# Holding the sums of squares behind the turned tokens in a two-layer decoder trunk

## The chip, the core and the metric

The kernel runs on one core of a Trainium2 chip. The metric is device time in microseconds (us) of one execution. Engines go by the profile's names: PE is TensorE (PEld its weight loads), DVE is VectorE, ACT is ScalarE, POOL is GpSimd, SP is the engine that issues most DMAs.

## The reference

Sixteen learned meta tokens are put ahead of 512 real ones, which gives 528 tokens of 2048 features in float32. Two layers follow. The first normalizes by the root mean square, projects, and runs multi-scale retention beside a complex diagonal state space (S5); the second does the same with gated linear attention. Each ends in an output projection and a residual sum, and a last normalization closes the trunk. The change concerns the first normalization alone:

```
def _rmsnorm(x, w):
    xf = x.astype(jnp.float32)
    y = xf * lax.rsqrt(jnp.mean(xf * xf, axis=-1, keepdims=True) + EPS)
    return (y * w.astype(jnp.float32)).astype(x.dtype)

h = concat(meta, x)                                   # (1, 528, 2048)
q, k, v, z_a, u, z_b = split(_rmsnorm(h, norm_ab_w) @ w_in_ab)
```

## The kernel before

The language used here takes a program written in plain order and lets a planner order the instructions of each engine: ready work first, earlier lines of the program first among the ready, and blocks marked with a high priority ahead of the rest. Each engine then runs its list in order. The planner also sets the waits.

The opening is this. Six tiles `xt` of 88 tokens x 2048 features are loaded in two halves of the features (L228 to L232), first the left halves of all six, then the right ones. For each of 16 blocks of 128 features (k) and each half of the tokens (hf), TensorE turns three tiles of 88 x 128 into one PSUM tile `pt` of 128 x 264 (L242; 96 transposes, 32 turned tiles). Four PSUM tiles rotate. ScalarE writes the high part `xh`, scaled by the norm's weight and rounded to the format of the fast passes (L245). VectorE writes the rest, `xl` (L246). A raw copy, by ScalarE for the first token half and VectorE for the second (L250, L252), goes to DRAM through POOL's queue (L253) for the residual sum later on.

The square root's part is kept out of the products: a projection is computed on unnormalized tokens, and its result is multiplied by `rb`, 1/rms of each token on all partitions. For `rb` the squares of each token are summed over whole rows of `xt`, three tiles on ScalarE (L262), three on VectorE (L260), written at the place in the program that follows the turning of the tokens and the copy of some weight vectors, `wv` (L256). Then come the mean (L263), the reciprocal root (`rsqrt`, L121 to L129), six small matmuls `pr` that spread it (L269) and two copies into `rb` (L271). The pool `p0` with the tokens is released behind them.

Products go by panels (`panel_steps`, L136): 128 columns of weights against all tokens, in four steps of four blocks. A step loads a weight tile `wr` (256 KB, L153, SP's queue), casts its high part on ScalarE (`wh`, L156), subtracts on VectorE (`wl`, L157), both with high priority, and issues 24 matmuls of 128 x 264 (L167). Three weight buffers and two accumulators rotate. The first panels are those of the S5 input; `u_out` multiplies an accumulator by `rb` (L298) and sets it free. Beside them VectorE computes the S5 parameters (L340 to L346 are helpers through which most of its work goes), which TensorE transposes (`pa`, L414; `pc`, L459; `pp`, L485) and later uses for small kernels (`pk`, L528). Their loads (L332 to L334, L443) use room that `p0` has left.

Of the kernel before, what the change touches and what calls it, by code (L numbers as in the profile page):

```python
# [13 lines left out]
AF = mybir.ActivationFunctionType  # L14
ALU = mybir.AluOpType
# [16 lines left out]
T = 8  # L32
# [9 lines left out]

# [1 line left out]
def host_tables():  # L44
# [33 lines left out]
def tile_hybrid(ctx: ExitStack, tc: tile.TileContext, d: dict, out: bass.AP, dbg=None):  # L78
# [20 lines left out]

# [1 line left out]
    cst = cpool.tile([P, P + GC], F32, name="cst")  # L101
# [16 lines left out]
    def rsqrt(pool, ms, shape, np_, tag):  # L118
        """(ms + eps) ** -0.5 for a small tile of mean squares"""
        v = pool.tile(shape, F32, name="rs_v", tag=tag + "v")  # L120
        V.tensor_scalar(v[:np_], ms, EPS, None, op0=ALU.add)  # L121
        y = pool.tile(shape, F32, name="rs_y", tag=tag + "y", bufs=2)
        V.tensor_scalar(y.bitcast(I32)[:np_], v.bitcast(I32)[:np_], -0.5, 1597463007.0, op0=ALU.mult, op1=ALU.add)
        for _ in range(3):
            t = pool.tile(shape, F32, name="rs_t", tag=tag + "t")
            V.scalar_tensor_tensor(t[:np_], y[:np_], -0.5, y[:np_], op0=ALU.mult, op1=ALU.mult)
            V.tensor_tensor(t[:np_], t[:np_], v[:np_], op=ALU.mult)
            y2 = pool.tile(shape, F32, name="rs_y", tag=tag + "y", bufs=2)
            V.scalar_tensor_tensor(y2[:np_], t[:np_], 1.5, y[:np_], op0=ALU.add, op1=ALU.mult)  # L129
            y = y2  # L130
        return y

# [1 line left out]
    WPRI = 3000  # L134

    def panel_steps(res, wsrc, row0, col, xs, tok0=0, x0=None):  # L136
        """psum [128, 2, 512] = W[row0:, col:col+128]^T @ xs, float32 through three exact passes"""
        nk = len(xs)
# [53 lines left out]

    # ================= tokens in, transposed, split =================
    NB = 6
# [62 lines left out]
    for t in range(NB):  # L257
        junk = p0.tile([TB, D], F32, name="junk", tag="junk", bufs=2)
        if t % 2:
            V.scalar_tensor_tensor(junk, xt[t], 1.0, xt[t], op0=ALU.mult, op1=ALU.mult, accum_out=ssq[:, t:t + 1])  # L260
        else:
            A.activation(junk, xt[t], AF.Square, accum_out=ssq[:, t:t + 1])  # L262
    V.tensor_scalar(ssq, ssq, 1.0 / D, None, op0=ALU.mult)  # L263
# [19 lines left out]

    # ================= S5 =================
    u_d = dpool.tile([NG * GC, T, NC8], F32, name="u_d")
# [32 lines left out]

    # -- discretization, on [32 pairs, (group parity, state)] --
    NQ = 32  # L320
# [58 lines left out]
    n = sm()  # L379
# [36 lines left out]

    # -- powers of a: pw[:, n, re/im, pair] --
    V.memset(pw[:, 0, 0, :], 1.0)
# [3 lines left out]
    def cmul(dst, a, b, n):  # L422
        """dst[n] = a[n] * b, complex on axis 2"""
        bb = [b[:, j:j + 1, :].to_broadcast([P, n, NPAIR]) if n > 1 else b[:, j:j + 1, :] for j in range(2)]
        for j in range(2):
            q = sd.tile([P, 4, NPAIR], F32, name="cm", tag="cm", bufs=2)[:, :n]
            tt(q, a[:, :, 1, :], bb[1 - j], ALU.mult)
            tt(dst[:, :, j, :], a[:, :, 0, :], bb[j], ALU.mult)
            tt(dst[:, :, j, :], dst[:, :, j, :], q, ALU.add if j else ALU.subtract)
# [8 lines left out]

    # -- discretized input matrix, output matrix transposed --
    bt = [sd.tile([P, NPAIR, GC], F32, name="bt", tag="tmp", bufs=3) for j in range(2)]  # L440
# [26 lines left out]

    # -- chunk-end states from within the chunk --
    def pwv(j, ps_):
# [22 lines left out]
    sk = sk_cm.__enter__()  # L492
    # -- kernel of the lags within a chunk, output matrices times powers --
    zero = sk.tile([P, T * GC], F32, name="zero")
# [56 lines left out]
    r0b = r0b_cm.__enter__()  # L551
    # -- states across chunks: slot c becomes the state after chunk c --
    for c in range(1, NC8 - 1):
# [52 lines left out]

    # ================= residual stream, output projection =================
    def out_proj_panel(wsrc, row0, os, m, tok0=0):
# [11 lines left out]
    def split(pool, src, n, tag, bufs, scale=None):  # L620
        """an operand as the exact sum of two parts that the fast passes carry"""
        oh = pool.tile([P, n], F32R, name="oh", tag=tag + "h", bufs=bufs)
        ol = pool.tile([P, n], F32R, name="ol", tag=tag + "l", bufs=bufs)
        A.copy(oh, src)
        tt(ol, src, oh.bitcast(F32), ALU.subtract)
        return oh, ol
# [4 lines left out]
    def stacked(pool, name, n):  # L631
        """a 16-row operand's parts on three row groups, zeros between: one fast pass makes the three products"""
        t = pool.tile([SK, n], F32R, name=name)
        V.tensor_copy(t, zcol[:SK].to_broadcast([SK, n]))
        return t

    def stack_a(t, src, scale=None):
        """rows (high, high, low)"""
        for rows in (S0, S1):
            if scale is None:  # L640
                A.copy(t[rows], src)
            else:
                A.activation(t[rows], src, AF.Copy, scale=scale)
        if scale is None:
            tt(t[S2], src, t.bitcast(F32)[S0], ALU.subtract)
        else:
            stt(t[S2], src, scale, t.bitcast(F32)[S0], ALU.mult, ALU.subtract)

    def stack_b(t, src):
        """rows (high, low, high)"""  # L650
        for rows in (S0, S2):
# [13 lines left out]

    # ================= retention =================
    def rope(col, decay=None):
# [20 lines left out]
    def ret_panels(hd, order="kqvvzz", after=lambda n: None):  # L688
        """a head's projections, one panel for each letter"""
        vtm = vtm3  # L690
# [32 lines left out]
    def ret_mix(hd, k_, q_, vt, vtm, sz):  # L723
        # keys, token-major, decayed to the end of their chunk
        kw = r0b.tile([P, NCH - 1, P], F32, name="kw", tag="kw", bufs=1)
# [5 lines left out]
        stack_a(kwm3, pt[:META, 3 * P:], kdecm[:META, hd:hd + 1])  # L731
        # scores, transposed: [key, query]
        st = r0b.tile([P, NCH, P], F32, name="st", tag="st", bufs=2)
# [9 lines left out]
        stack_a(stm3, stm)  # L743
        # states and outputs, token-major
        on = r0b.tile([P, NCH, RDV], F32, name="on", tag="on", bufs=1)
# [100 lines left out]

    # ================= S5: gelu, gated linear unit =================
    r1p_cm = tc.tile_pool(name="r1p", bufs=1, side="right", reuse_waits="tile")
# [70 lines left out]

    # ================= layer 1: gated linear attention =================  # L920
    w_in = d["w_in_c"][0]
# [4 lines left out]

    # -- the low-rank gate code: the weights' high parts, then their low parts, in two passes --
    accg = psm.tile([P, 2, 512], F32, name="accg", tag="mm")
# [7 lines left out]
    opool_cm.__exit__(None, None, None)  # L936
    # -- 1 / rms of every token, along the free axis on all partitions --
    pq = mx("pq")
# [40 lines left out]
    def last_weights(f4):  # L979
        """the last projection's weights, split, where the tokens were"""  # L980
        for k in range(4):
# [9 lines left out]
    def last_norm():  # L991
        """the final norm's weight on all partitions"""
        for f4, (tag, bufs) in enumerate((("k", 2), ("k", 2), ("b", 2), ("b", 2))):
# [3 lines left out]
    def turn_group(f4):  # L997
        """the residual of 512 features, token-major, in place: chunk c in tile 4 f4 + c"""
        pts = []
# [11 lines left out]
    def evac(parts, src):  # L1011
        """a value, or its high and its low part"""
        if len(parts) == 1:
# [5 lines left out]
    def products(o, pairs):  # L1019
        """the sum of a^T b, of values in float32 or through the parts that the fast passes carry"""  # L1020
        todo = []
# [39 lines left out]
    for hd in range(GH):  # L1061
        # gates: cumulative log decay (times 16) within every chunk
        bs = []
# [34 lines left out]
        if done is not None:  # L1098
            O = gate(*done)
        # scores [key, query]: every pair of positions in the level where they part  # L1100
        st = gt("st", "st", 1, [P, SEQ])
# [29 lines left out]
        for lv, sz in enumerate((64, 32, 16, 8, 4, 2)):  # L1131
# [22 lines left out]
            place(sz, lv, pl)  # L1154
        # decays to the chunk's end for keys, from its start for queries
        parts = 2 if hd < GH - 1 else 1
# [45 lines left out]
        for z in zs:  # L1202
            A.activation(z, z, AF.Silu)
        # states and outputs, token-major
        if parts == 2:
# [53 lines left out]

    # ================= last projection, token-major; final norm =================  # L1260
    ssq = gt("ssq", "ssq", 1, [P, NCH, 4])
# [51 lines left out]
```

## Time and profile before

| what | value |
|---|---|
| time, median of 3 runs | 2174.68 us (2173.01 to 2177.08) |
| span of the profiled execution | 2173.9 us |
| PE busy | 2106.5 us, 97% |
| DVE busy | 1160.2 us, 53% |
| ACT busy | 803.2 us, 37% |
| moved by DMA | 223.72 MB, mean 103 GB/s |

The profiled execution lies inside the three runs: no other time of it is told than its span, which is 0.8 us below the median. The busy share of PE is an average over the whole run; its first slices are thinner than the rest, and those are the ones to look into.

### The profile page before, as it was taken

What the parts mean: (1) busy time and instruction counts of PE and PEld (TensorE: products, weight loads), DVE (VectorE), ACT (ScalarE), POOL (GpSimd) and SP (SyncE); (2) the same over time, 40 slices, a digit from 0 to 9 for tenths busy, and PEclk for the clock granted to TensorE, in tenths of its full rate; (3) what the DMA queues carried; (4) which work ended last, traced back from release to release, by engine and by line L of the source; (5) the groups of instructions that cost most, each with busy time, mean ns of one, the idle gap of its engine ahead of it and who ended that gap; (6) DMA issues with size and microseconds to landing.
All of it is one profiled execution on the core that took longest, in us unless ns stands there. A gap on an engine that the chain in (4) does not pass through costs nothing.

```text
span 2173.9 us, 39751 instructions
## 1 busy us (share of the span) xinstructions
PE 2106.5 (97%) x16052; PEld 1947.0 (90%) x16052; DVE 1160.2 (53%) x2452; ACT 803.2 (37%) x1536; POOL 71.7 (3%) x110
## 2 busy tenths in 40 slices
PE   6998988999999999999999999999999999999998
PEld 5997887999999999999999998988798889889776
DVE  5886871534344433445444566545834573555376
ACT  5333422543332333234323354344325333533343
POOL 3100012000000000000000020000000000000000
PEclk9999998999999999999999999999999999999999
DMA  7855437652323222322333322223232223233232
GB/s 232 216 119 146 135 96 238 194 164 78 89 74 92 78 79 86 90 77 80 93 92 92 93 80 73 79 68 83 78 88 68 83 79 88 68 83 89 82 117 78
DMA packets 391374, 223.72 MB, mean 103 GB/s; under 512 B 45990, under 2 KB 375030, under 8 KB 391062
## 3 DMA queue, kind: packets, MB, share of 16 engines
q1 hardware_dynamic: 383062, 208.10, 34.0%
q0 software_dynamic: 8096, 13.07, 2.2%
q8 instruction: 126, 2.06, 0.4%
q14 instruction: 58, 0.48, 0.1%
q10 hardware_dynamic: 32, 0.01, 0.0%
HBM read 193.15 MB, written 27.92 MB: 102 GB/s over the span
## 4 chain that ended last, share of the span: by engine, by line
PE 81%; issue 8%; DMA 4%; DVE 3%; ACT 2%; SPq 1%; POOL 0%; ACTq 0%; DVEq 0%; POOLq 0%
PE acc L167 69%; PE last L1271 2%; PE po L1029 2%; PE pl L1152 1%; DMA x_d<-St 1%; DMA xt<-in_x_dram 1%; DVE wl L157 1%; PE pkv L1029 1%; DMA y_d<-Y 1%; PE po L767 1%; DMA wr<-in_w_out_c_dram 1%; PE po L766 1%; ACT wh L156 1%; PE pkv L758 0%; DMA wr<-in_w_in_ab_dram 0%
## 5 line engine op out<-in xcount | busy, mean ns | idle before, releaser
L156 ACT CAST wh<-wr 128x512 fp32r<-128x512 f32 x608 | 375.7, 620 | 1011.0 <-PE acc L167 872.5
L167 PE MATMUL acc<-xh,wh 128*128 128x264 f32 (+1 forms) x3200 | 734.6, 300 | 3.6 <-ACT wh L156 3.6
L167 PE MATMUL acc<-xh,wl 128*128 128x264 f32 (+1 forms) x3200 | 730.7, 299 | 7.5 <-DVE wl L157 7.5
L167 PE MATMUL acc<-xl,wh 128*128 128x264 f32 (+1 forms) x3200 | 729.3, 299 | 0.0
L157 DVE TENSOR_TENSOR wl<-wr,wh 128x512 fp32r<-128x512 f32 x608 | 417.1, 687 | 543.4 <-ACT wh L156 522.5
L167 PEld LDWEIGHTS acc<-xh,wl 128*128 128x128 f32 x3200 | 509.4, 189 | 29.4 <-DVE wl L157 12.1
L167 PEld LDWEIGHTS acc<-xh,wh 128*128 128x128 f32 x3200 | 510.9, 189 | 23.6 <-ACT wh L156 4.8
L167 PEld LDWEIGHTS acc<-xl,wh 128*128 128x128 f32 x3200 | 513.1, 189 | 19.4 <-issue 0.4
L167 PE MATMUL acc<-oh,wh 128*128 128x264 f32 x896 | 181.9, 284 | 0.5 <-DVE sz L343 0.5
L167 PE MATMUL acc<-oh,wl 128*128 128x264 f32 x896 | 181.8, 284 | 0.0
L167 PE MATMUL acc<-ol,wh 128*128 128x264 f32 x896 | 181.8, 285 | 0.0
L343 DVE TENSOR_TENSOR h<-acc,h 128x528 f32<-128x528 f32 (+1 forms) x144 | 100.9, 700 | 143.8 <-PE acc L167 143.3
L167 PEld LDWEIGHTS acc<-oh,wh 128*128 128x128 f32 x896 | 139.0, 189 | 0.7 <-issue 0.7
L167 PEld LDWEIGHTS acc<-ol,wh 128*128 128x128 f32 x896 | 138.7, 188 | 0.0
L167 PEld LDWEIGHTS acc<-oh,wl 128*128 128x128 f32 x896 | 138.7, 188 | 0.0
L343 DVE TENSOR_TENSOR vf<-acc,rb 128x528 f32<-128x528 f32 x32 | 22.6, 707 | 44.8 <-PE acc L167 44.7
L912 POOL TENSOR_TENSOR sqa<-sqa,s 128x528 f32<-128x528 f32 x13 | 17.3, 1329 | 883.8 <-ACT s L911 883.8
L1141 ACT ACTIVATE E<-E 128x512 f32<-128x512 f32 x48 | 29.7, 629 | 32.8 <-DVE E L343 32.6
L343 DVE TENSOR_TENSOR E<-b 128x256 f32<-128x256 f32 (+1 forms) x112 | 41.0, 409 | 0.0
L1152 PEld LDWEIGHTS pl<-qh,E 128*64 128x64 f32 x704 | 26.3, 137 | 12.2 <-issue 4.3
L343 DVE TENSOR_TENSOR E<-E,k 128x512 f32<-128x512 f32 (+1 forms) x56 | 36.3, 668 | 0.0
L242 PE MATMUL pt<-cst,xt 88*128 88x88 f32 x96 | 17.0, 315 | 16.8 <-DMA xt<-in_x_dram 8.9
(430 smaller groups left out, 2147.3 us busy)
## 6 DMA issues: line engine op xcount, KB each, us to landing
wr<-in_w_in_ab_dram SPq DMA_DIRECT2D x256, 256.0 KB
wr<-in_w_in_c_dram SPq DMA_DIRECT2D x192, 256.0 KB
wr<-in_w_out_ab_dram SPq DMA_DIRECT2D x96, 256.0 KB
wr<-in_w_out_c_dram SPq DMA_DIRECT2D x64, 256.0 KB
xT_d<-raw POOLq DMA_DIRECT2D x32, 132.0 KB, 3.7
h<-xT_d SPq DMA_DIRECT2D x16, 264.0 KB
k_d<-zero SPq DMA_DIRECT2D x8, 512.0 KB
ca_d<-CA SPq DMA_DIRECT2D x32, 128.0 KB
```

Of the source, the lines that this page charges most:

```text
L156: A.copy(wh, wr)
L157: V.tensor_tensor(wl, wr, wh.bitcast(F32), op=ALU.subtract)
L167: PE.matmul(o, a[:, k, :], b[:, cols], start=(kk == 0 and pi == 0), stop=(kk == nk - 1 and pi == 2))
L242: PE.transpose(pt[:, j * TB:(j + 1) * TB], xt[hf * 3 + j][:, k * P:(k + 1) * P], ident[:TB, :TB])
L343: V.tensor_tensor(o, a, b, op=op)
L766: PE.matmul(po[:, :RDV], st[:, c, :], vt[:, c, :], start=True, stop=False)
L767: PE.matmul(po[:, :RDV], q_[:, toks(c)], S, start=False, stop=True)
L912: (G if m < KT - 2 else V).tensor_tensor(sqa, sqa, s, op=ALU.add)
L1029: PE.matmul(o, a, b, start=(n == 0), stop=(n == len(todo) - 1))
L1141: A.activation(e, e, AF.Exp, scale=1.0 / 16)
L1152: PE.matmul(pl[r:r + 64, c * 64:(c + 1) * 64], kh[j][:, c * P + r:c * P + r + 64], qh[j][:, c * 64:(c + 1) * 64], start=(j == 0), stop=(j ...
L1271: PE.matmul(acc, a[:, cs_], b, start=(k == 0 and pi == 0), stop=(k == 3 and pi == 2))
```

## The change

Each of the six instructions that square a token tile is handed to `keep_in_program_order`. The call adds an edge of order, without a wait, from the instruction to the one that the program traced just before it on the same engine. For the first square on ScalarE that is the last `xh` (L245, block 15, second half), for the first on VectorE the copy of `wv` (L256), and for the others the square before them on their engine. The planner may no longer put a square earlier in an engine's list. Before, it was free to do so once the token tile was loaded.

```
@@ -257,9 +257,10 @@
     for t in range(NB):
         junk = p0.tile([TB, D], F32, name="junk", tag="junk", bufs=2)
         if t % 2:
-            V.scalar_tensor_tensor(junk, xt[t], 1.0, xt[t], op0=ALU.mult, op1=ALU.mult, accum_out=ssq[:, t:t + 1])
+            i = V.scalar_tensor_tensor(junk, xt[t], 1.0, xt[t], op0=ALU.mult, op1=ALU.mult, accum_out=ssq[:, t:t + 1])
         else:
-            A.activation(junk, xt[t], AF.Square, accum_out=ssq[:, t:t + 1])
+            i = A.activation(junk, xt[t], AF.Square, accum_out=ssq[:, t:t + 1])
+        tc.keep_in_program_order(i)
     V.tensor_scalar(ssq, ssq, 1.0 / D, None, op0=ALU.mult)
     rs = rsqrt(cpool, ssq, [TB, NB], TB, "rs0")
```

The other hunks of the diff only take comments out. Line numbers behind L262 grow by one.

## Rows read from the trace of the kernel before

**Rows 1.** The page, part 1: busy us, share of the span, instructions.
```profile
PE 2106.5 (97%) x16052; PEld 1947.0 (90%) x16052; DVE 1160.2 (53%) x2452; ACT 803.2 (37%) x1536; POOL 71.7 (3%) x110
```
**Rows 2.** The chain that ended last, first 100 us: start us, us, what.
```profile
13.56 13.50 DMA xt<-in_x_dram
27.05 1.74 ACT junk L262
...
32.15 3.37 PE acc L167 x15
...
47.47 4.91 PE acc L167 x39
```
**Rows 3.** Busy us (instructions) by stretch: PE, PEld, DVE, ACT, POOL; clock, DMA share, GB/s.
```profile
20.45:30.24 9.79, 3.64 (x19) 2.62 (x19) 8.09 (x14) 8.96 (x16) 2.81 (x7) 1.00 0.94 324
30.24:36.00 5.76, 5.76 (x31) 5.76 (x30) 4.38 (x10) 3.09 (x9) 2.57 (x5) 1.00 0.96 341
...
47.00:60.00 13.00, 12.59 (x103) 12.17 (x102) 11.06 (x35) 2.68 (x6) 2.91 (x9) 1.00 0.47 147
60.00:72.40 12.40, 12.40 (x106) 12.40 (x104) 11.60 (x56) 4.66 (x8) 0.00 (x0) 1.00 0.81 156
```
**Rows 4.** The same for instructions on the turned tiles pt alone: PE, PEld, DVE, ACT.
```profile
0.00:17.50 17.50, 3.73 (x15) 2.29 (x15) 2.10 (x5) 2.83 (x7) 1.00 0.66 170
17.50:20.45 2.95, 2.90 (x15) 2.18 (x15) 2.61 (x8) 1.99 (x5) 1.00 1.01 301
20.45:30.24 9.79, 3.64 (x18) 2.61 (x18) 3.84 (x10) 3.34 (x9) 1.00 0.94 324
...
0.00:60.00 60.00, 17.01 (x96) 12.36 (x96) 19.71 (x48) 19.18 (x48) 1.00 0.70 219
```
**Rows 5.** The instructions that square the tokens: duration ns min/median/max, first and last start.
```profile
L262 ACT ACTIVATE junk<-xt x3: 1896/1897/1898, 20.2 to 27.0; 88x2048 f32<-88x2048 f32 x3
L260 DVE SCALAR_TENSOR_TENSOR junk<-xt x3: 2276/2277/2280, 20.7 to 48.9; 88x2048 f32<-88x2048 f32 x3
L262 ACT ACTIVATION_READ_ACCUMULATOR junk<-xt x3: 188/190/190, 22.0 to 28.8; 88x1 f32 x3
L260 DVE DVE_READ_ACCUMULATOR junk<-xt x3: 78/78/80, 22.9 to 51.2; 88x1 f32 x3
```
**Rows 6.** The timeline of SP's queue: start us, us, what it issued.
```profile
15.89 6.89 SPq L153 DMA_DIRECT2D wr<-in_w_in_ab_dram  x3
22.83 0.59 SPq L233 DMA_DIRECT2D cst<-in_cst_dram  x1
...
58.31 0.33 SPq L332 DMA_DIRECT2D lr<-in_s_lam_re_dram  x1
```
**Rows 7.** SP's waits from 15 to 31 us: total us, times, longest us.
```profile
SPq L153 <- DMA wr<-in_w_in_ab_dram: 5.3, 1, 5.3
```
**Rows 8.** The timeline of all engines where the products begin.
```profile
29.57 0.61 ACT L156 CAST wh<-wr 128x512 fp32r<-128x512 f32 x1
...
30.24 0.81 PE L167 MATMUL acc<-xh,wh 128*128 128x264 f32 x2
```
**Rows 9.** The timeline of DVE around rb; in brackets idle time before and its releaser.
```profile
48.81 0.21 DVE L256 COPY wv<-pv 128x64 f32<-128x64 f32 x1
48.94 2.28 DVE L260 SCALAR_TENSOR_TENSOR junk<-xt 88x2048 f32<-88x2048 f32 x1
...
58.32 0.43 DVE L271 COPY rb<-pr 128x264 f32<-128x264 f32 x1 [0.32 <-PE pr L269]
...
60.53 1.16 DVE L298 TENSOR_TENSOR ut<-acc,rb 128x264 f32<-128x264 f32 x2 [0.38 <-PE acc L167]
```
**Rows 10.** The timeline of PE at two later stops.
```profile
73.78 0.24 PE L414 MATMUL pa<-cst,abf 32*128 32x32 f32 x1 [1.11 <-DVE abf L343]
...
170.48 0.60 PE L528 MATMUL pk<-CA,bbD 128*32 128x128 f32 x2 [7.34 <-DVE CA L343]
```
**Rows 11.** Busy us by stretch around the second stop, columns as in rows 3.
```profile
165.00:170.00 5.00, 0.00 (x0) 0.00 (x0) 1.83 (x4) 0.88 (x2) 0.00 (x0) 0.54 0.60 111
170.00:175.00 5.00, 4.52 (x20) 4.16 (x21) 2.83 (x5) 1.81 (x3) 0.00 (x0) 0.50 0.42 104
```

More of the change, by code (lines that the diff above doesn't have):

```diff
@@ L259, in tile_hybrid @@
         if t % 2:
-            V.scalar_tensor_tensor(junk, xt[t], 1.0, xt[t], op0=ALU.mult, op1=ALU.mult, accum_out=ssq[:, t:t + 1])
+            i = V.scalar_tensor_tensor(junk, xt[t], 1.0, xt[t], op0=ALU.mult, op1=ALU.mult, accum_out=ssq[:, t:t + 1])
         else:
-            A.activation(junk, xt[t], AF.Square, accum_out=ssq[:, t:t + 1])
+            i = A.activation(junk, xt[t], AF.Square, accum_out=ssq[:, t:t + 1])
+        tc.keep_in_program_order(i)
     V.tensor_scalar(ssq, ssq, 1.0 / D, None, op0=ALU.mult)
```

## The prediction

> **What bounds the kernel now.** I read the page first, then the chain of waits over the first 100 us, then busy times by stretch, then the instructions one by one. The page says that TensorE is busy 97% of the span [rows 1], so as a whole the kernel is bound by products, and only a stage in which TensorE stands still can give much. The change touches such a stage. From 20.45 to 30.24 us TensorE works 3.64 of 9.79 us, while ScalarE works 8.96 and VectorE 8.09; from 30.24 to 36 and from 60 to 72.4 it has no gap at all, and from 47 to 60 only 0.41 us [rows 3]. So whatever is won or lost before 30 us is carried by TensorE up to 72 us.
>
> What fills ScalarE in the thin stretch? The three squares there cost 1.90 + 0.19 us each, the two on VectorE (L260, the third stands at 48.94) 2.28 + 0.08 us each [rows 5, 9]: 6.27 us of ScalarE's 8.96 and 4.72 us of VectorE's 8.09. TensorE's transposes need the PSUM tiles that these two engines empty, so each square holds the transposes up.
>
> But the squares are not the only thing that is late there. The chain shows the tokens' DMA still landing until 27.06 us (13.56 + 13.50) and a square right behind it [rows 2]. And the weights are late too: SP issues the first three weight tiles from 15.89 on and the tables at 22.83, is free at 23.42, and its next weight load then waits 5.3 us for a weight tile to land [rows 6, 7], so the first weights are in SBUF at about 28.8 us. ScalarE casts them at 29.57 and the first product can follow at 30.24 [rows 3, 8]. The squares delay this cast by 0.8 us at most.
>
> **The change, part by part.** Nothing is added or removed: the same six squares, the same DMAs. The mark ties each square to the instruction traced just before it on its engine, by order alone: ScalarE's first to the last scaled copy of a turned tile, VectorE's first to the copy of the weight vectors (L256), the others each to the last one before. Three things follow.
>
> *1. The thin stretch.* 6.27 us of ScalarE and 4.72 us of VectorE come free between 20 and 29 us. A turned tile (three transposes) costs ScalarE 19.18/32 = 0.60 us, VectorE 19.71/32 = 0.62 us and TensorE 3 x 17.01/96 = 0.53 us [rows 4]. In the run before, 15 + 15 + 18 = 48 transposes, 16 of 32 tiles, are through by 30.24 us [rows 4]. Free of squares the three could take 17 tiles (eight feature blocks, both halves, and one half of the ninth) before the last token block lands at 27.06; the 18th needs that block. From then on at 0.62 us a tile there is room for four more by 29.57. So at the first product the lead is between 1 tile (the planner puts the casts first) and 5 tiles (17 + 4 - 16); the rows do not tell which, and I take 3. For TensorE that is 3 x 0.53 = 1.6 us fewer transposes among the products behind 30.24 us (1 tile 0.5, 5 tiles 2.7).
>
> *2. The start of the products.* It can move 0.8 us ahead (29.57 against 28.8) if ScalarE is free when the weights land. It can also move back: more tiles done early means more copies of the raw tile (132 KB each) sent to DRAM while tokens and weights arrive. The DMA engines moved 324 GB/s at a share of 0.94 in that stretch [rows 3], so four more copies are 4 x 132 KB / 324 GB/s = 1.6 us if the weights stand behind all of them, nothing if they pass. I take 0 between -0.8 and +1.6. The Trainium skill (DMA: Bandwidth & Descriptors, Issuing engines are not separate DMA queues) says that transfers started by different engines end on the same 16 DMA engines and interleave, which speaks against this change; by it the start would lie at the later end, and this trace, with its 0.94, does not contradict it.
>
> So TensorE reaches the end of the second panel some 1.6 us earlier; bounds: 2.7 + 0.8 = 3.5 earlier, and 1.6 - 0.5 = 1.1 later.
>
> *3. The squares in their new place.* On ScalarE three squares come after the last tile, from about 47 us on, where it works 2.68 of 13 us [rows 3]: hidden. On VectorE they are not. The scale of the tokens (rb) hangs on all six squares: L256 ends its wait at 48.81, the one square follows at 48.94, and rb is complete at 58.75 [rows 9]. Two more squares in that line cost 4.72 us. The lead gives some back: from 30.24 to 48.81 the 16 remaining tiles took 18.57/16 = 1.16 us each [rows 4, 9], so 3 tiles fewer bring L256 3.5 us forward. Net: rb 4.72 - 3.5 = 1.2 us later (lead 1 tile: 3.6 later; 5 tiles: 1.1 earlier). What stands behind rb: the first panel's output (L298), which at present waits 0.38 us for TensorE [rows 9], and the release of the token buffers, behind which SP issues the loads of the S5 parameters at 58.31 [rows 6]; SP's later weight loads stand behind those. VectorE then works 11.60 of 12.40 us [rows 3], so a lateness there is not caught up.
>
> TensorE first notices at its transposes of the discretized S5 parameters: there it already waits 1.11 us, until 73.78, for VectorE [rows 10]. If its instructions stand in the same order, it throws away its lead of 1.6 us and waits the 1.2 us on top: +1.2 us. If the planner, which orders the whole stretch anew, puts products into that gap, the lead is kept: -1.6 us. Without a reason for either I take the middle, -0.2 us, on the median of 2174.68: 2174.5 us. (The profiled execution had a span of 2173.9 us; what lies around it is taken as unchanged.)
>
> **The clock.** The stretches print a granted clock of 1.00 from the start [rows 3], but the products from 32.15 us on take 3.37/15 = 0.22 us each and those from 47.47 us on 4.91/39 = 0.13 us [rows 2], nearly the ratio of TensorE's two levels; so I read the first products, from 30.24 to about 35.5 us, as running at 1.2 GHz. If the denser transposes bring the rise to 2.4 GHz forward, at most half of these 5.3 us is won, 2.7 us; if not, nothing. I take nothing; it lies inside the bounds. The Trainium skill (TensorE: Matmul & The Clock Gate, What's actually happening) says that the throttled state is the default and activity releases it; by that rule some of the 2.7 us would come, and no run here shows how much.
>
> **Rivals.**
>
> *The lead counts in full (faster).* ScalarE's 6.27 us really were the brake, TensorE starts its products 0.8 us earlier with five tiles behind it, and the clock rises with them: 2.7 + 0.8 + 2.7 = 6.2 us, 2168.5 us. For it: TensorE idles 6 us in the thin stretch [rows 3]. Against: tokens to 27.06, weights to 28.8 [rows 2, 7], neither of which a square delays. Chance 0.12.
>
> *The squares become the line to rb (slower).* This decides when L256 does not come forward at all, because the planner keeps TensorE's transposes mixed with products as before. Then rb, L298 and the S5 loads are 4.72 us later, VectorE has no slack to win it back, and TensorE stops at the third panel's accumulator and at L414: 2174.68 + 4.7 = 2179.4 us, with a few more products behind it up to 2181. It turns into a loss as soon as L256 moves forward by less than 4.72 us, and one that can be measured only when it hardly moves. For it: VectorE's 11.60 of 12.40 us. Chance 0.15.
>
> *A later stop falls differently.* At 163 to 170 us TensorE stands 7.34 us for VectorE [rows 10] and is then granted 0.54 and 0.50 of its clock, the lower level, until 175 us [rows 11]. A new order could remove the stop (7.34 plus half of the 5 us at the lower clock: 2164.8 us) or add its like (2184.5 us). Against it: the change lies 100 us ahead, and both engines have the same work in between. Chance 0.05 each way.
>
> *It does nothing.* The third VectorE square is already behind all tiles; if the planner delays the rest of the stretch to match, every end stays: 2174.7 us. Chance 0.05.
>
> **How the numbers follow.** The forecast (-1.6 to +1.2, with bounds of -3.5 and +3.6) has 0.58. All of it lies within 0.2%, 4.35 us, about what a measurement of this kernel can tell from no change. Same: 0.58 + 0.05 = 0.63. Faster by more: 0.12 + 0.05 = 0.17. Slower by more: 0.15 + 0.05 = 0.20. The range takes in the first two rivals, 2168.5 and 2181, and leaves out the two of the late stop: 2168 to 2181.5. The forecast alone would be 2171.2 to 2178.3.
>
> **What would show it.** In the profile after: no L262 or L260 between 20 and 29 us; more than 48 transposes by the first product, which still starts between 29.4 and 31.9 us; three squares in a row on VectorE behind L256; rb complete near 60 us; the wait at L414 near 3.9 us, or filled. It is wrong if the first product starts well before 29 us, if L256 stays at 48.8 us, or if the stop at 163 us is gone.

## The result, and the profile after

The change makes the kernel slower: 2184.36 us (median of 4 runs, 2182.04 to 2188.4) against 2173.85 us (4 runs, 2172.23 to 2177.08), ratio 1.0051 [1.0037, 1.0066]. Forecast were 2174.5 us, no measurable change, and a range that ended at 2181.5: both were missed. Behind line 262 the changed kernel's line numbers are one higher.

The squares went where they were sent. The view of the instructions on junk, of the kernel after, has none before 46 us, and TensorE has 63 transposes behind it at its first product, against 48 (second fence: the windows of tile pt, columns as in [rows 4]):

```profile
L262 ACT ACTIVATE junk<-xt x3: 1911/1917/1918, 46.3 to 51.3; 88x2048 f32<-88x2048 f32 x3
L260 DVE SCALAR_TENSOR_TENSOR junk<-xt x3: 2277/2281/2289, 47.6 to 53.3; 88x2048 f32<-88x2048 f32 x3
```
```profile
0.00:33.66 33.66, 13.29 (x63) 9.27 (x63) 11.99 (x29) 11.78 (x30) 1.00 0.79 241
```

The stretch up to the first product answers to the first one of [rows 3]: TensorE works 6.64 us of 13.21, where it worked 3.64 of 9.79 (windows, after):

```profile
20.45:33.66 13.21, 6.64 (x34) 4.80 (x34) 7.05 (x19) 7.29 (x20) 5.89 (x11) 1.00 0.93 323
33.66:39.60 5.94, 5.94 (x31) 5.94 (x31) 3.75 (x8) 2.61 (x7) 2.68 (x5) 1.00 0.92 315
```

But the first product comes at 33.66 us and not at 30.24 [rows 8], behind ScalarE's cast of the first weights at 32.98. By the single records of the traces the first weight tile lands at 30.04 us and not at 28.75, and the cast follows 2.9 us behind it instead of 0.8, because four scaled copies (xh) and a raw copy stand ahead of it in ScalarE's list, with waits of 0.94 and 0.79 us for TensorE (timeline of ScalarE, after):

```profile
31.88 1.22 ACT L245 ACTIVATE xh<-pt,wv 128x264 fp32r<-128x264 f32 x3 [0.79 <-PE pt L242]
32.98 1.14 ACT L156 CAST wh<-wr 128x512 fp32r<-128x512 f32 x2
```

The timeline of VectorE, after, shows a wait in the thin stretch that the kernel before has not, and then the line to rb that answers to [rows 9]:

```profile
24.28 0.43 DVE L250 COPY raw<-pt 128x264 f32<-128x264 f32 x1 [2.97 <-DMA xT_d<-raw]
...
47.46 0.21 DVE L256 COPY wv<-pv 128x64 f32<-128x64 f32 x1
47.59 2.28 DVE L260 SCALAR_TENSOR_TENSOR junk<-xt 88x2048 f32<-88x2048 f32 x1
...
53.30 2.29 DVE L260 SCALAR_TENSOR_TENSOR junk<-xt 88x2048 f32<-88x2048 f32 x1 [0.27 <-ACT junk L262]
...
63.25 0.42 DVE L272 COPY rb<-pr 128x264 f32<-128x264 f32 x1
```

L256 comes 1.35 us forward, and rb is complete at 63.67 us (63.25 + 0.42), 4.9 us later than the 58.75 of before. None of this has cost TensorE anything yet. The windows (columns as in [rows 3]) of the kernel before, then of the kernel after, show where the time goes:

```profile
36.00:100.00 64.00, 61.07 (x498) 58.78 (x497) 52.80 (x173) 27.22 (x63) 14.22 (x28) 1.00 0.80 212
100.00:125.00 25.00, 24.62 (x200) 23.71 (x199) 25.00 (x43) 8.92 (x15) 0.00 (x0) 1.00 0.63 153
...
315.00:400.00 85.00, 73.12 (x897) 69.39 (x895) 20.15 (x38) 23.54 (x57) 16.91 (x26) 0.90 0.77 244
```
```profile
36.00:100.00 64.00, 62.66 (x495) 60.61 (x495) 53.36 (x170) 28.22 (x56) 10.68 (x22) 1.00 0.75 210
100.00:125.00 25.00, 15.66 (x113) 15.45 (x111) 13.24 (x22) 6.17 (x14) 1.94 (x4) 0.80 0.69 116
...
315.00:400.00 85.00, 72.25 (x936) 68.49 (x935) 25.33 (x56) 20.32 (x45) 21.68 (x32) 0.98 0.75 228
```

From 36 to 100 us TensorE does 495 matmuls against 498: the lead of 15 transposes has paid for the late start. From 100 to 125 it does 113 against 200, with 9.0 us less busy time and a granted clock of 0.80. The timeline of TensorE, after, has one row for it, and ScalarE's says what it waited for:

```profile
79.46 0.24 PE L415 MATMUL pa<-cst,abf 32*128 32x32 f32 x1 [0.69 <-DVE abf L344]
...
113.24 1.12 PE L460 MATMUL pc<-cst,cl 128*128 128x128 f32 x4 [9.34 <-ACT cl L457]
```
```profile
112.78 0.40 ACT L457 COPY cl<-cl 128x256 f32<-128x256 f32 x1 [10.19 <-DMA cl<-in_s_c_im_dram]
```

So the new stop is a wait for a DMA: the fourth and last load of cl (128 KB of the S5 output matrices), for which TensorE's transposes and ScalarE's copy stand in line. The timelines of SP's queue, before and after, and of GpSimd's queue, before and after, show what has changed about this load:

```profile
91.49 2.29 SPq L455 DMA_DIRECT2D cl<-in_s_c_im_dram  x2
```
```profile
93.59 0.64 SPq L456 DMA_DIRECT2D cl<-in_s_c_re_dram  x1
...
98.80 1.14 SPq L456 DMA_DIRECT2D cl<-in_s_c_im_dram  x1
```
```profile
93.63 5.02 POOL L305 DMA_DIRECT2D U<-u_d  x8 [34.65 <-DMA u_d<-ut]
```
```profile
96.92 5.02 POOL L306 DMA_DIRECT2D U<-u_d  x8 [33.62 <-DMA wr<-in_w_in_ab_dram]
```

Before, the fourth cl load is issued at 93.41 us (its row covers two issues and ends at 93.78), 0.22 us ahead of the first of eight U loads; after, it is issued 1.88 us behind it. From the single records of the trace, issue and last landing:

```
load               before           after
cl, fourth         93.41   97.16    98.80  112.70
weights, next to   93.89  100.36    97.78  111.43
U, first           93.63   98.47    96.92  102.63
U, eighth          98.02  107.53   101.31  112.54
```

The load takes 13.9 us instead of 3.75. That the two changed places is a matter of a few microseconds: the first cl load slid by 5.25 us (88.34 to 93.59) and the fourth by 5.39, along with rb and the S5 parameters, while the U loads, which hang on the fourth u panel (the fourth panel of the S5 input), slid by 3.3 us only. The stop brings a second loss, as the known one at pk does in [rows 11] (windows, after):

```profile
105.00:110.00 5.00, 0.00 (x0) 0.00 (x0) 0.18 (x1) 0.00 (x0) 0.00 (x0) 0.79 1.12 132
110.00:115.00 5.00, 1.76 (x8) 1.76 (x9) 0.55 (x1) 1.00 (x3) 0.00 (x0) 0.50 0.63 112
115.00:120.00 5.00, 5.00 (x32) 5.00 (x31) 3.58 (x7) 1.21 (x3) 0.00 (x0) 0.69 0.34 107
```

The granted clock is at its lower level, 1.2 GHz, from about 108 to 118 us, and TensorE works from 113.24 on: 4.9 us at half the pace lose 2.4. With the 9.0 us less busy time that makes 11.4 us. Matching the two traces matmul by matmul (the nth on each tile, medians) gives about the same: TensorE is 0.5 us ahead of the kernel before at 95 to 100 us, 10.8 us behind at 120 to 125, and 12.0 behind at 310. Some of it comes back in this pair of profiles, whose spans differ by 6.4 us (2180.3 and 2173.9): TensorE is 8.0 us behind at 390 us, 7.2 at 500 and 6.4 at the end. Between 315 and 400 us the kernel before has waits of 3.5, 3.2 and 3.0 us, where the longest after is 2.2, and the mean clock of 0.98 instead of 0.90 stands for 3.4 us at the lower level instead of 17. The profiled execution was the fastest of the four after, and the other three had spans of 2182.6 to 2186.6 us, so the part given back differs between executions; the medians differ by 10.5 us.

### The profile page after: what moved, and what is told of

Same layout as the page of the kernel before. It is cut to its first block, busy times and chain, and to the rows that moved or that the text cites. A ratio compares the mean times of both kernels' runs of the same rounds, so it can differ in the third digit from the quotient of the medians.

```text
span 2180.3 us, 39750 instructions
## 1 busy us (share of the span) xinstructions
PE 2104.9 (97%) x16052; PEld 1944.9 (89%) x16052; DVE 1160.2 (53%) x2452; ACT 803.8 (37%) x1536; POOL 71.7 (3%) x110
## 4 chain that ended last, share of the span: by engine, by line
PE 82%; DVE 7%; DMA 5%; ACT 3%; issue 2%; SPq 1%; ACTq 0%; DVEq 0%
PE acc L167 70%; PE last L1272 2%; PE po L1030 2%; DVE wl L157 2%; PE pl L1153 1%; DMA wr<-in_w_in_ab_dram 1%; DMA ca_d<-CA 1%; PE pkv L1030 1%; DVE St L561 1%; SPq L536 1%; ACT wh L156 1%; DMA cl<-in_s_c_im_dram 1%; DVE sc L558 1%; DVE sc L560 1%; PE po L768 1%
## 5 line engine op out<-in xcount | busy, mean ns | idle before, releaser
L157 DVE TENSOR_TENSOR wl<-wr,wh 128x512 fp32r<-128x512 f32 x608 | 416.8, 687 | 533.1 <-ACT wh L156 515.1
```

The lines of the kernel that those rows point to most:

```text
L157: V.tensor_tensor(wl, wr, wh.bitcast(F32), op=ALU.subtract)
```

## The experiments

Four runs were first made to tell two readings of this apart: "late line" (rb and all behind it 5 us late) and "late start" (the first product 3.4 us late). A third, "crossing", came out of them: only the place of the fourth cl load against the first U loads counts. Each is compared with the kernel before on the same chip.

**ScalarE's squares alone** (in the loop of the squares):

```diff
-        tc.keep_in_program_order(i)
+        if t % 2 == 0:
+            tc.keep_in_program_order(i)
```


> Only ScalarE's three squares are held; VectorE's are free as before. Theory 'late line' (VectorE's two further squares make rb late, the S5 parameters follow late, and the last load of the output matrix meets the loads of U): VectorE squares two tiles early again, rb complete near 59 to 60 us, the last of the four loads (cl) issued before the first load of U, no stop above 2 us at the transposes pc, time within 0.2% of before (2170 to 2178). Theory 'late start' (the cast of the first weights stands behind the turned tiles and the first product starts 3.4 us later): the first product still starts at 33 us or later and the time stays near 2180 to 2184.

2186.66 us, 1.0050 [1.0038, 1.0063]: the whole loss. VectorE's free squares were put behind the tiles by the planner all the same (47.9 to 53.6 us), so it is not half of the change but all of it; the first product (34.24 us) and rb (63.99) are late as well, and the run does not tell the two readings apart. The fourth cl load was issued 2.65 us behind the first U load. TensorE's waits from 95 to 125 us:

```profile
PE pc L461 <- ACT cl L458: 10.8, 3, 8.7
```

**VectorE's squares alone:**

```diff
-        tc.keep_in_program_order(i)
+        if t % 2:
+            tc.keep_in_program_order(i)
```


> Only VectorE's three squares are held; ScalarE's are free as before. Late line: three squares in a row behind L256, rb 4 to 5 us later than before, the last cl load behind the first load of U, a stop of 8 to 10 us at pc and 2182 to 2186. Late start: the first product stays near 30 to 31 us, as ScalarE's order has its three squares ahead of the first cast, and the time goes back to 2172 to 2177.

2174.91 us, 0.9997 [0.9987, 1.0006]: nothing lost. The planner left one of ScalarE's squares at 20 us and put two behind. The first product comes at 31.70 us, and rb is complete at 62.49, 3.7 us late: a line almost as late as in the changed kernel, at no cost. (By the first cl load, at 90.18 us, 1.8 us of the lateness are left.) As the start is only 1.5 us late here, the time alone would fit "late start" too. Here the fourth cl load is issued 0.07 us ahead of the first U load (94.44 and 94.51; timeline of SP's queue, then TensorE's waits from 90 to 125 us):

```profile
94.44 0.38 SPq L457 DMA_DIRECT2D cl<-in_s_c_im_dram  x1
```
```profile
PE pc L461 <- ACT cl L458: 0.7, 2, 0.6
```

**Buffers of their own for cl, in the changed kernel.** The cl loads wait for buffers that they share with the loads and products of the S5 input matrix (tag tmp), the fourth for one that an earlier cl load has to leave; four buffers take these waits away:

```diff
-            cl = sd.tile([P, 4, 2, NP], F32, name="cl", tag="tmp", bufs=3)
+            cl = sd.tile([P, 4, 2, NP], F32, name="cl", tag="cl", bufs=4)
```


> The kernel after, with buffers of their own for the four loads of S5's output matrix (cl), so that none waits for a buffer. Late line: all four land before the loads of U start, the stop of 9.34 us at pc and the 10.2 us at the lower clock behind it are gone; 2184.4 less 9.3 and 2.4 gives 2172 to 2175. Late start: the stop may go, but the 3.4 us at the start and what follows from them stay: not under 2178.

2177.5 us, 1.0006 [0.9997, 1.0015]. The cl loads are issued from 75.26 to 78.99 us, the U loads from 97.67 on, and TensorE has no wait at pc. The time lies between the two forecasts, with the kernel before at 2176.76 on this chip. The squares, the first product (33.46 us) and rb (62.80 us) are nearly as late as in the changed kernel (33.66 and 63.67). So the late start and the late line together are worth at most 0.15% here, and the stop is the rest (that the buffers give nothing of their own is the last experiment). With the loads, the planner moved the last transposes of cl on TensorE forward too, from behind 474 products to behind 325.

**A late rb without the change.** The kernel before, with VectorE squaring two tiles of tokens a second time, in order, behind the others:

```diff
+    for t in (1, 3):
+        junk = p0.tile([TB, D], F32, name="junk", tag="junk", bufs=2)
+        i = V.scalar_tensor_tensor(junk, xt[t], 1.0, xt[t], op0=ALU.mult, op1=ALU.mult, accum_out=ssq[:, t:t + 1])
+        tc.keep_in_program_order(i)
-    V.tensor_scalar(ssq, ssq, 1.0 / D, None, op0=ALU.mult)
+    i = V.tensor_scalar(ssq, ssq, 1.0 / D, None, op0=ALU.mult)
```


> The kernel before, its early squares kept, with two more squares on VectorE between L256 and the mean (they write the same sums again), so rb is late by 4.7 us and nothing ahead of 48 us changes. Late line: the stop at pc appears, 5 us or more with a lower clock behind it, and 2181 to 2186. Late start: no first product is late, so at most the 1 to 2 us that VectorE's lateness costs directly: 2174 to 2176.

2190.86 us, 1.0067 [1.0054, 1.0081]. The start is that of the kernel before (first product at 30.14 us), rb is complete at 65.76, 7.0 us late. The fourth cl load (102.58) falls 2.34 us behind the first U load (100.24), and TensorE's waits from 100 to 130 us hold the same stop:

```profile
PE pc L463 <- ACT cl L460: 11.0, 3, 10.2
```

By itself this run fits "late line" as well as "crossing". The next one separates them.

**The same late rb with four buffers for cl** (both edits above).

> The kernel before with two more squares on the line to rb (rb some 7 us late), as the run with the late rb, and besides that four buffers of their own for cl. Theory 'crossing': the lateness stays and costs little, the cl loads are issued before 85 us, far ahead of the U loads, no stop at pc; 2174 to 2180 against 2190.9 without the buffers. Theory 'late line': about 2190 again.

2179.88 us, 1.0023 [1.0013, 1.0034]. rb is 5.2 us late (63.90; 1.9 us less than without the buffers), the cl loads are issued by 81.7 us, and TensorE waits 0.2 us at pc. Of 0.67% some 0.44 went, most of it with the crossing; 0.23%, 5 us, stayed. The trace shows a place where lateness itself costs: TensorE waits at the spreading of rb and then for an accumulator that L298 has not yet set free (L302 here), and works on at the lower clock (TensorE's waits from 40 to 95 us, then a window):

```profile
PE pr L273 <- DVE rsb L272: 1.8, 2, 1.5
PE acc L167 <- DVE ut L302: 1.3, 1, 1.3
```
```profile
65.00:70.00 5.00, 5.00 (x24) 5.00 (x24) 2.57 (x15) 0.06 (x1) 0.00 (x0) 0.50 0.75 153
```

Matched with the kernel before, TensorE falls back by some 4 us between 55 and 75 us. The same two waits stand in the run without the buffers, where it falls back by some 3 us there and by some 12 at pc. The changed kernel has neither: from 40 to 95 us it waits 0.7 us, at L415 alone. So "late line" is a real loss where the products start early and rb is late, but not the loss of this change.

**The U loads out of the way.** First, the changed kernel with the eight early U loads written behind the eighth panel:

```diff
-        if m % 4 == 3:
-            gs = slice((m - 3) * 8, (m + 1) * 8)
+        if m == 7:
+            for n in (3, 7):
+                gs = slice((n - 3) * 8, (n + 1) * 8)
...
```


> The changed kernel with the first eight U loads issued together with the second eight (behind the eighth u panel), so that no U load stands near the fourth cl load, which is as late as before that edit. Theory 'crossing': the fourth cl load takes about 4 us, the stop at pc is 1 us or less, the clock is not lowered there, and the time is 2174 to 2179 unless the later U loads lengthen the stop at pk. Theory 'late line': still 2182 to 2188.

2186.52 us, 1.0050 [1.0037, 1.0064], and it tells no more of the theories than the changed kernel: the planner put the first eight U loads back to 96.88 us, since their data were there, and the fourth cl load again stood behind them (99.44), with a stop of 9.19 us. So the U loads were tied to the data instead, each over all eight panels:

```diff
-        if m % 4 == 3:
-            gs = slice((m - 3) * 8, (m + 1) * 8)
+        if m == 7:
             for t in range(T):
-                dmab(U[t * GC:(t + 1) * GC, gs],
-                     u_d[(m - 3) * P:(m + 1) * P, t, :].rearrange("(g h) c -> h g c", h=GC))
+                dmab(U[t * GC:(t + 1) * GC],
+                     u_d[:, t, :].rearrange("(g h) c -> h g c", h=GC))
```


> The changed kernel with the sixteen U loads (eight behind the fourth u panel, eight behind the eighth) made into eight, each over all eight u panels, so that none can be issued before the eighth panel is out (about 164 us). TensorE's instructions stand in the same order as in the changed kernel: the last four transposes of cl behind 474 products. Theory 'crossing': the fourth cl load, issued at 98.8 us again, lands in about 4 us instead of 13.9, TensorE's stop at pc (9.34 us) shrinks to under 2 us, the clock is not lowered at 108 to 118 us, and 9 to 12 us come back by 125 us; the time is 2173 to 2178, more only if the later U loads are then waited for. Theory 'late line': the line to rb is as late as it was, so 2182 to 2187.

TensorE's order up to the last transposes of cl (behind 474 products) and SP's up to the fourth cl load are those of the changed kernel, and that load is issued at the same time, 98.83 us. It now lands at 102.34, after 3.5 us instead of 13.9, and the stop is gone (windows, and TensorE's waits from 95 to 125 us):

```profile
100.00:125.00 25.00, 24.41 (x202) 23.68 (x200) 23.92 (x41) 10.15 (x20) 0.00 (x0) 1.00 0.44 122
```
```profile
PE pc L459 <- ACT cl L456: 0.7, 2, 0.4
```

202 matmuls in this stretch, 200 in the kernel before, 113 after; at 120 to 125 us TensorE is 0.6 us ahead of the kernel before, where the changed kernel is 10.8 us behind. Nothing but the U loads is gone from this stretch, so they are the cause of the stop. The time as a whole is 2206.1 us, 1.0140 [1.0123, 1.0156], far outside what either theory gave: the later U loads seem to do the same to another transfer. Issued from 153 us on, they land in 6 to 21 us; VectorE waits 21.5 us for a copy of CA to ca_d to land, and TensorE's stop at pk [rows 10] grows from 7.34 to 19.63 us (VectorE's waits from 160 to 185 us, then TensorE's timeline):

```profile
DVE kt L346 <- DMA ca_d<-CA: 21.5, 1, 21.5
```
```profile
182.92 0.61 PE L528 MATMUL pk<-CA,bbD 128*32 128x128 f32 x2 [19.63 <-DVE CA L343]
```

That explains some 12 of the 31 us; the rest comes later, with waits of TensorE of 6.3, 8.4 and 7.1 us between 338 and 386 us, and was not followed.

**Both in one queue.** The changed kernel with the cl loads issued by GpSimd, in the order of the program with the first U loads, and so ahead of them:

```diff
-            dma(cl[:, :, 0, :], csrc[mg * 4:mg * 4 + 4].rearrange("m q p -> q m p"))
+            tc.keep_in_program_order(dmab(cl[:, :, 0, :], csrc[mg * 4:mg * 4 + 4].rearrange("m q p -> q m p")))
...
+                if m == 3:
+                    tc.keep_in_program_order(i)
```


> The changed kernel with the four cl loads issued on GpSimd's queue, in the order of the program, so that they stand ahead of the first U loads in one queue; the planner may set other work anew (here the last transposes of cl stand behind 439 products instead of 474). Theory 'crossing': no stop of over 2 us at pc and no lowered clock there; 2173 to 2180. Theory 'late line': 2182 to 2187.

2178.17 us, 1.0014 [1.0003, 1.0025]. The fourth cl load at 96.17, the first U load at 96.91; pc costs TensorE 3.7 us in four waits, the longest 2.1, and the clock stays up there. Most of the loss is back, with the squares still pinned (first product at 32.83 us, rb at 61.82).

**A crossing without lateness.** The kernel before with its fourth cl load issued by GpSimd behind the first U loads:

```diff
+    def c_turn(j, mg, behind=False):
...
+    for j, mg in ((0, 0), (0, 1), (1, 0)):
+        c_turn(j, mg)
...
         u_out(m, panel(w_in, 0, C_U + m * P, xhl))
+        if m == 3:
+            c_turn(1, 1, behind=True)
```


> The kernel before, its squares as they were, with one thing changed: the fourth load of cl is issued by GpSimd behind the first eight U loads instead of by SyncE ahead of them, and its copy, transposes and two copies to CT come behind it. Nothing at the start or on the line to rb is late. Theory 'crossing' (the late line costs time only because the fourth cl load falls behind the first U loads): the first product stays at 30.2 us and rb at 58.8, the load takes 10 us or more instead of 3.75, TensorE stops at pc for about as long as in the changed kernel (5 to 10 us), the granted clock falls behind it, and the time is 2181 to 2188. Theory 'late line' (5 us of lateness at rb are handed to everything behind it): no lateness, so 2174 to 2176. If the planner places the transposes themselves later on TensorE, the stop is smaller and the run says less.

2210.25 us, 1.0161 [1.0147, 1.0175], and not the test it was meant to be. The load, issued at 97.31 us behind the U loads, takes 11.2 us with nothing late, as expected; but the planner set its transposes at 150 us, so TensorE does not stop for it there, and stops at pk instead, from 223 to 252 us, 24 us in sum. It shows the load's delay, not the stop.

**Sixteen raw buffers in the changed kernel.**

```diff
-            raw = p0.tile([P, HALF], F32, name="raw", tag="raw", bufs=8)
+            raw = p0.tile([P, HALF], F32, name="raw", tag="raw", bufs=16)
```


> The changed kernel with sixteen raw buffers instead of eight, so that VectorE's raw copies wait less for the copies to xT_d. If these waits hold the start of the products (33.66 us against 30.24), the first product comes at 31 to 32 us and VectorE reaches the last turned token some 2 us sooner. Theory 'crossing': the time goes by whether the fourth cl load still falls behind the first U load, so 2180 to 2186 if it does and 2173 to 2178 if it does not. Theory 'late line': 1 to 3 us below the changed kernel, in step with rb. If the order of the casts on ScalarE holds the start, nothing moves.

2185.36 us, 1.0048 [1.0031, 1.0064], no better than the change itself. The waits of the raw copies are gone, and 2.0 of the 3.4 us of the late start with them: first product at 31.62 us, L256 at 44.39, rb complete at 60.61, 3.1 us ahead of the changed kernel. The fourth cl load is still issued 2.83 us behind the first U load (97.01 and 94.18), and the stop is there (TensorE's waits from 95 to 125 us):

```profile
PE pc L460 <- ACT cl L457: 9.9, 3, 8.7
```

The stop came though start and rb are earlier: for "crossing". Against a small "late line" or "late start" the run says nothing. In the profiles TensorE is 8.9 us behind the kernel before at 300 us, where the changed kernel is 12.0 behind, so about 3 us were won; behind 315 us they are lost again (11.6 behind at 500 us), and the interval of the ratio is too wide to tell 3 us from nothing.

**Four buffers for cl elsewhere.** In the kernel before, and with VectorE's squares alone pinned:

> The kernel before with four buffers of their own for cl, so that its loads wait for none. In the kernel before the fourth load was issued 0.2 us ahead of the first U load and its stop was small, so by theory 'crossing' there is little to gain: 2172 to 2176. Rival: the loads wait for buffers on a line that sets the end; then 2165 to 2171.

> VectorE's squares alone pinned, and four buffers of their own for cl. By theory 'crossing' no load crosses the U loads and the pc stop stays away with a margin: 2172 to 2177, as the run with VectorE's squares alone. By theory 'late line' the same 2 to 5 us above the kernel before.

2173.77 us, 0.9996 [0.9987, 1.0005], and 2179.05 us, 1.0016 [1.0007, 1.0025]. Where nothing crosses, the buffers win nothing. The second misses the forecast of "crossing" and lies in that of "late line": it has a new wait of 3.4 us at pp for VectorE, with which TensorE goes from 0.6 us behind the kernel before (105 to 110 us) to 4.6 (120 to 125). Why VectorE is late there was not followed. No version beat the kernel before by a measurable amount.

The runs by the place of the load, without the two whose loss lies at pk and behind it (the U loads over all panels, and the crossing without lateness):

```
run                    cl behind U, us   longest stop at pc   ratio
before, four buffers   -25               0.2                  0.9996
vector alone           -0.1              0.6                  0.9997
before                 -0.2              0.9                  1
after, four buffers    -19               none                 1.0006
after, one queue       -0.7              2.1                  1.0014
vector, four buffers   -19               0.2                  1.0016
late rb, four buffers  -18               0.2                  1.0023
after, sixteen raw     +2.8              8.7                  1.0048
scalar alone           +2.7              8.7                  1.0050
after, U written later +2.6              9.2                  1.0050
after                  +1.9              9.3                  1.0051
late rb                +2.3              10.2                 1.0067
```

## Why the prediction was wrong

**The step that failed** is the rival "a later stop falls differently", to which the prediction gave 0.05 for each sign, with "the change lies 100 us ahead, and both engines have the same work in between". In the sum everything behind L414 stood at nothing, on that argument alone. What came in its place is a new stop of 9.34 us at pc and 4.9 us at the lower clock, 11 us in all. The rival's price ("its like" added, 2184.5 us) is near the 2184.36 measured, but that is luck: it was taken from the pk stop, which stayed where it was, and half of the new loss came back behind 315 us in the profiled execution and, by their spans, less in the others. The argument was wrong at two points. The next place that can stop TensorE is not the pk stop at 163 us but pc at 97 us, where the kernel before waits 0.92 us and the fourth cl load is issued with 0.22 us to spare; the prediction shows no row of the stretch from 74 to 163 us. And the work in between is the same, but its order against the DMA queues is not: of two chains that the change delays by different amounts (the cl loads by 5.4 us, the U loads by 3.3), the more delayed one had the small margin and fell behind the other.

**The thin stretch** (step 1) was right in kind: 63 transposes against 48 are 15, five tiles, the upper bound of the lead. They paid for a start that was 3.4 us late and no more, as the 495 and 498 matmuls by 100 us show.

**The start of the products** (step 2) was mis-sized: +3.4 us against bounds of -0.8 and +1.6. The prediction named the copies to xT_d as contenders for the DMA engines, and the first weights do land 1.3 us later, inside its 1.6. The other 2.1 us are the cast, which stands further behind the landing; here the prediction let ScalarE be free, and did not count the eight raw buffers that the copies to xT_d hold: VectorE's raw copies waited 3.9 us for them in three waits. With sixteen buffers 2.0 us came back; the weights then land 0.4 us later than before, and the cast comes 1.8 us behind them. The Trainium skill (DMA: Bandwidth & Descriptors, Issuing engines are not separate DMA queues) says that transfers started by different engines interleave on the same 16 DMA engines; the later landing agrees with that.

**The line to rb** (step 3) was mis-sized: L256 came 1.35 us forward instead of 3.5, and with sixteen raw buffers 4.4, so the missing part went with the waits for the copies to xT_d; rb +4.9 us against bounds of -1.1 and +3.6. That is the "squares become the line to rb" rival's lateness of 4.7, but not its price: its stop at L414 did not come (0.69 us instead of 1.11: these transposes now stand behind 304 products instead of 269), and four buffers show the lateness as worth 0.06% here. The stop at the third panel's accumulator that this rival named did come in the two runs with a late rb and an early start, where it cost 3 to 4 us. The two squares cost more than their 4.72 us as well: from L256 to the mean it takes 9.3 us instead of 3.0, because weight subtractions (L157) and a raw copy stand between and behind the squares.

**The clock** did not rise earlier: in the first six us of products TensorE did 31 instructions in both kernels [rows 3].

**The pk stop** at 163 us stayed (8.1 instead of 7.3 us), as forecast. Of the signs listed one failed early on: the first product was to start between 29.4 and 31.9 us. The sign that mattered was in no list: a short wait with a near neighbour in another queue.

## What to carry to other kernels

When work is moved, list the waits behind it that end on a DMA with a short margin, and ask of each which transfers on other queues it will stand behind once it is a few microseconds late: here 2 us of order between two queues cost ten, where 4 to 5 us of plain lateness cost 0 to 5. A load that waits for a buffer can be moved out of reach by buffers of its own (here four instead of three shared ones), without reordering the source; what else the planner then moves has to be read from the profile. And an edit to the source order proves nothing under a planner until the issue times in the profile after have been read.

## What the runs showed of the hardware

- Eight U loads of 132 KB from GpSimd's queue hold what SP issues just behind the first of them. A 128 KB load issued 1.9 us behind it took 13.9 us, and 3.5 us without the U loads; issued 0.07 us ahead of it (VectorE's squares alone), 4.5 us. A 256 KB weight load (issued 97.78 and 97.30) took 13.7 and 4.6 us, but only 6.5 us when issued 0.26 us behind the first U load (kernel before). Which part of this is the queue and which the shared DMA engines was not separated. From 105 to 110 us of the kernel after, the DMA share is 1.12 at 132 GB/s, where it was 0.94 at 324 GB/s from 20.45 to 30.24 us of the kernel before [rows 3]: with these loads under way, the engines are full at less than half the rate.
- What a stop costs through the clock hardly depends on its length. Behind all 23 stops of TensorE of more than 6.5 us in the traces it worked 3.3 to 5.8 us at the lower level, so each lost 1.6 to 2.9 us more: 5.2 us behind one of 7.34 us (pk, before), 3.6 behind one of 8.11 (pk, after), 4.9 behind one of 9.34 (pc, after), 5.8 behind one of 19.63 (pk, with one U load).
